# Strassen weight sums of a decoder layer: their loads and stores on GpSimd's queue, three buffers, an earlier load, and one half chunk less look-ahead

## The chip, the cores and the metric

The kernel runs on one core of a Trainium2 chip. A core has five engines that work side by side, each in its own order: TensorE (PE in the profile; its weight loads are PEld), VectorE (DVE), ScalarE (ACT), GpSimd (POOL) and SyncE (SP, which here only issues DMAs). The engines and the DMAs wait for each other by semaphores. The metric is the device time of one execution in microseconds, lower is better.

## The reference

One layer of a decoder on 256 tokens of width 2048, in float32. The parts, cut to what matters:

```python
h = rms_norm(x, attn_norm_g)
q, k, v, p = split(h @ w_in)                  # 3 x 1024 for 8 heads, 1024 for pooling
a = moba_attention(rms_norm(q), rms_norm(k), v, rel_bias)
m = multiscale_pool(p, pool_w, pool_scale)    # causal means over 2, 4, 8, 16 tokens
x = x + concatenate([a, m]) @ w_out
u = rms_norm(x) @ w_up                        # 2048 x 11264
y = conv_b + sum(conv_w[i] * shifted(u, i) for i in range(3))
gate, val = split(y)
x = x + (silu(gate) * val) @ w_down           # 5632 x 2048
```

With 256 tokens, all keys lie in one block, so the attention is plain causal attention with a bias.

## The kernel before

Every weight is used once, so the kernel is a stream of weights. A *step* is one half chunk of weights, 128 partitions by 1024 float32 columns; a chunk of two half chunks is one DMA of 1 MB into a `raw` tile (four of them, `RAWS`), issued by SP. TensorE multiplies in a reduced format, so each half chunk is split in two parts that are multiplied one after the other: ACT copies `raw` to `wh` (L169), DVE subtracts to get `wl` (L170). Activations are split in the same way. `split(i)` makes the part pair of half chunk i; `AHEAD` says how many half chunks the splits run ahead of TensorE, and `wpool` has `AHEAD + 1` buffers of `wh` and `wl`.

The order on all engines is written out by hand. The main loop at the end goes over the steps: first the splits that are due, then the step's matmuls, then its hooks, small pieces of work that `after(u, f)` hung on step u. Each engine does its share of this in that order. The steps:

- 0 to 47: six *token blocks* of eight steps for v, k and q (`tok_half`, L207). Attention hangs on them as hooks. At step 17 the attention's bias rows go out to DRAM as `band` and come back as `T`, both by POOL's queue.
- 48 to 63: the pooling columns (`feat_half`, L238 for `wh` with both activation parts, L240 for `wl` with one). 64 to 97: the output projection, which ends in the residual `x2`, its square sums on POOL (L638, L662) and, two steps into the next stage, `stats2`: a matmul `ps_row` (L348) that sums over partitions, from which the row scale `rrow` comes. `x2_T` transposes the residual on TensorE (L645).
- From step 98 (`UP0`) on, three *thirds* (`THIRDS`). Each has an up-projection, eight steps for each group of 256 hidden columns (four for the gate, a *gate block*, four for the value, a *value block*), and a down-projection. After each block comes its tail: `conv` (ACT L468, DVE `fs` L469, `u` L682, three taps on `y` L687 to L690), then for the gate the SiLU (L696), and for the value the product with the gate and its split into `hid` (L713 to L723). In the first half of a third's groups the tail also forms the seven combinations of the hidden columns for Strassen's scheme (*Strassen value blocks*).

Strassen's scheme replaces eight products of half-size blocks of `w_down` by seven, for which sums of weight blocks are needed. For 44 pairs of blocks (`NJ`) the kernel makes these sums itself, as *jobs*: `job_load` reads the four blocks (`job <- in_pairs`, 512 KB), `job_sums` makes four additions on DVE (L194), `job_store` writes the sums to DRAM (`tsum <- job`, 512 KB), from where the weight stream reads them in the down-projection (`raw <- tsum`). There is one `job` tile. The jobs are hung on *free* steps: 12 to 31, 64 to 97 and all steps of the up-projections. Job k takes the five free steps from the 5k-th on: load after the first, sums after the third, store after the fifth. Loads and stores stand in SP's queue among the weight loads.

Of the kernel before, what the change touches and what calls it, by code (L numbers as in the profile page):

```python
# [35 lines left out]
F32 = mybir.dt.float32  # L36
# [5 lines left out]
P = 128  # L42
D = 2048
S = 256
# [9 lines left out]
L = 384  # L54
CH = 2048
HALF = CH // 2
AHEAD = 5
RAWS = 4
BH = 768

# [4 lines left out]
UP0 = 98  # L65
# [43 lines left out]
def layer(ctx: ExitStack, tc: tile.TileContext, xT, wts, pairs, par, relT, ident_d, onehot_d, icnt_d, out):  # L109
    nc = tc.nc  # L110
    ctx.enter_context(tc.manual_schedule())
    keep = ctx.enter_context(tc.tile_pool(name="keep", bufs=1))
    wpool = ctx.enter_context(tc.tile_pool(name="wpool", bufs=AHEAD + 1))
    mm = ctx.enter_context(tc.tile_pool(name="mm", bufs=2, space=bass.MemoryType.PSUM))
# [11 lines left out]
    def small(name):  # L126
        return sm.tile([P, 512], F32, name=name, tag="small")
# [9 lines left out]
    offset, n = {}, 0  # L137
# [7 lines left out]
        first_part.setdefault(u, i)  # L145
    raws, wparts, tsum = {}, {}, {}

    def load(c, pieces=1, j=0, queue=None):

        if c not in raws:  # L150
            raws[c] = wpool.tile([P, CH], F32, name="raw", tag="raw", bufs=RAWS)
        r, k = raws[c], sched[chunk[c][0]]
        if k is None:
            w = HALF * len(chunk[c])
            o, n = j * w // pieces, w // pieces
            src = bass.AP(tensor=wts.tensor, offset=wts.offset + offset[c] + o, ap=[[w, P], [1, n]])
            (queue or nc.sync).dma_start(r[:, o:o + n], src)
        else:
            nc.sync.dma_start(r[:, :BH], pairs[k][:, HALF - BH:])
            nc.sync.dma_start(r[:, BH:BH + HALF], tsum.pop(k))  # L160
# [11 lines left out]
    def split(i):  # L172
        u, k = parts[i]
        split_piece(u, k, 0, HALF if sched[u] is None or k else BH)
        if u == chunk[chunk_of[u]][-1] and (k or sched[u] is None):
            release(chunk_of[u])

    def release(c):

        raws.pop(c)  # L180
        if c + RAWS < len(chunk):
            load(c + RAWS)


    job = {}

    def job_load(k):
        job["t"] = keep.tile([P, 4, S], F32, name="job", tag="job")
        nc.sync.dma_start(job["t"], pairs[k].rearrange("p (a n) -> p a n", n=S))

    def job_sums(k):
        t = job["t"]
        for o, a, b in ((1, 0, 1), (0, 0, 2), (2, 1, 2), (3, 2, 3)):
            nc.vector.tensor_tensor(t[:, o, :], t[:, a, :], t[:, b, :], op=OP.add)  # L194

    def job_store(k):
        tsum[k] = dram.tile([P, HALF], F32, name=f"tsum{k}")
        nc.sync.dma_start(tsum[k].rearrange("p (a n) -> p a n", n=S), job.pop("t"))

    def tok_half(u, act, k0, ps, first, last):  # L200

# [63 lines left out]
    def load_xT(k0, k1):  # L265

        c = slice(KT + k0 * S if k0 else 0, KT + k1 * S)
        nc.sync.dma_start(xboth[:, c], xT[:, c])

    def x_split(k0, k1):  # L270
        for k in range(k0, k1):
            g = xboth[:, k:k + 1]
            nc.scalar.activation(xh[:, k, 0, :], xin[:, k, :], AF.Copy, scale=g)
            nc.vector.scalar_tensor_tensor(xh[:, k, 1, :], xin[:, k, :], g,
                                           xh[:, k, 0, :].bitcast(F32), op0=OP.mult, op1=OP.subtract)

    nc.vector.memset(ones, 1.0)
    load(0, 4, 0, nc.scalar)  # L280
    ps = small("ps_start")
    for _ in range(7):
        nc.tensor.matmul(ps[:, :P], ones, ones, start=True, stop=True)
    nc.scalar.preload_act_table_set("natural_log_exp_and_others")

    for k in range(4):
        load_xT(k, k + 1)
        if k:
            load(0, 4, k)
    for u in range(2, 8):  # L290
        load_xT(2 * u, 2 * u + 2)
        load(u // 2, 2, u % 2)
# [3 lines left out]
    for c in range(2):  # L296
        release(c)
    for u in range(4, AHEAD):
        x_split(2 * u, 2 * u + 2)
# [266 lines left out]
    def after(u, f):  # L566

        hooks.append((u, f))
# [11 lines left out]

    for u in range(AHEAD, 8):
        pre[u - AHEAD] = lambda u=u: x_split(2 * u, 2 * u + 2)
    for a in range(4):
# [11 lines left out]
    for b in range(2):  # L595
# [3 lines left out]
        at = st["q", b, "end"] + 3  # L599
# [40 lines left out]
    def x2_T(i):  # L640

        t, k0 = i % NT, i // NT * 4
        ps = small("ps_x2t")
        for k in range(4):
            nc.tensor.transpose(ps[:, k * P:(k + 1) * P], late["x2"][:, k0 + k, t * P:(t + 1) * P], ident)  # L645
        nc.scalar.activation(late["x2t"][:, t, k0 * P:(k0 + 4) * P], ps, AF.Copy)
# [25 lines left out]
    f0 = len(steps)  # L672
# [72 lines left out]
                nc.sync.dma_start(out[:, ts, cs], x)  # L745

    HIDF = max(f * 14 * P + (g1 - g0 - f) * 4 * S for g0, g1, f in THIRDS)
    free = [*range(12, 32), *range(64, UP0)]
    for n, (g0, g1, f) in enumerate(THIRDS):
        free += range(len(steps), len(steps) + 8 * (g1 - g0))  # L750
        for g in range(g0, g1):
# [1 line left out]
            steps += feat_block(lambda: late["h"], XK, lambda ps, n=n, j=g - g0: value(ps, n, j))  # L753
        steps += down_order([down_block(n, b, n == 2) for b in range(D // 512)])
    for i in range(8):
        after(f0 + 1 + i // 2, lambda i=i: x2_T(i))
    for k in range(NJ):
        at = free[5 * k:]
        after(at[0], lambda k=k: job_load(k))
        after(at[2], lambda k=k: job_sums(k))  # L760
        after(at[4], lambda k=k: job_store(k))

    for u, f in hooks:
        steps[u].append(f)
    assert len(steps) == len(sched) and f0 == UP0, (len(steps), len(sched), f0)
    done = AHEAD
    for u in range(len(steps)):
        if u in pre:
            pre[u]()
        while done < min(first_part[u] + AHEAD + 1, len(parts)):  # L770
            split(done)
# [83 lines left out]
```

## Time and profile before

| | |
|---|---|
| median of three runs | 1199.75 us (1199.39 to 1199.9) |
| profiled execution | 1199.44 us, of which span 1197.6 us |
| mean granted TensorE clock | 0.952 |
| busy share of the span: PE, DVE, ACT, POOL | 90%, 71%, 47%, 5% |
| DMA | 263.96 MB, mean 220 GB/s |

How to read it: a row of waits says who waited for whom, the microseconds in total, how often and the longest. In a row of a group of instructions, the figures after the bar are its busy time, the mean of one in ns, and the idle time of its engine just before them with what ended it. A row of the timeline has its start from the beginning of the span, its length, and in brackets the idle time before it. A row of DMA issues has how many, the size of each, and the median time from issue to landing. The letter q after an engine's name means its queue (sequencer). A busy TensorE is not one at its peak, since matmuls are pipelined, and its clock is at times granted only at half speed.

### The profile page before, as it was taken

How to read it: one execution, taken by the hardware profiler on the slowest of the kernel's cores; microseconds unless marked ns; L12 is line 12 of the kernel's file. 1: busy time of each engine (PE TensorE's matmuls, PEld its weight loads, DVE VectorE, ACT ScalarE, POOL GpSimd, SP SyncE). 2: the span in 40 equal slices, each digit the busy share in tenths (PEclk: the TensorE clock that was granted, in tenths of full speed). 3: DMA queues.
4: the chain of work that ended last, by engine and by line, in shares of the span. 5: the costliest groups of instructions: out<-in, count | busy, mean ns of one | idle time of the engine just before them, and what ended most of it. 6: DMA issues, size and time to landing. Idle time of an engine off the chain costs nothing.

```text
span 1197.6 us, 15090 instructions
## 1 busy us (share of the span) xinstructions
PE 1080.0 (90%) x5836; PEld 927.5 (77%) x5836; DVE 850.9 (71%) x1187; ACT 564.7 (47%) x750; POOL 54.8 (5%) x44
## 2 busy tenths in 40 slices
PE   9968899999969989897899998898789999898898
PEld 7756688878858867776798887777678988786787
DVE  6815656875666787677788667768677867877885
ACT  7523354455345444443555434444355644544652
POOL 0300003501010000000000000000000000000000
PEclk9988899999989998998899998989989999998899
DMA  9767654476665657575777655647478765664583
GB/s 358 256 133 232 210 177 147 149 267 235 231 216 176 222 180 249 182 242 163 282 282 276 224 212 191 213 166 255 163 259 303 268 248 184 241 239 164 202 302 117
DMA packets 53865, 263.96 MB, mean 220 GB/s; under 512 B 6312, under 2 KB 7112, under 8 KB 34208
## 3 DMA queue, kind: packets, MB, share of 16 engines
q1 hardware_dynamic: 52656, 260.11, 61.9%
q0 software_dynamic: 992, 2.63, 1.4%
q8 instruction: 45, 0.74, 0.2%
q10 hardware_dynamic: 144, 0.26, 0.1%
q14 instruction: 28, 0.23, 0.1%
HBM read 236.23 MB, written 26.74 MB: 220 GB/s over the span
## 4 chain that ended last, share of the span: by engine, by line
PE 38%; DMA 26%; DVE 25%; ACT 4%; issue 4%; SPq 1%; POOL 1%; DVEq 0%; ACTq 0%; POOLq 0%
DMA job<-in_pairs 13%; DMA tsum<-job 12%; DVE wl L170 11%; PE ps_down L217 10%; PE ps_down L231 8%; PE ps_feat L238 8%; PE ps_tok L207 6%; PE ps_feat L240 4%; DVE job L194 4%; DVE y L690 2%; ACT wh L169 2%; DVE y L688 2%; DVE u L682 2%; DVE fs L469 1%; ACT y L687 1%
## 5 line engine op out<-in xcount | busy, mean ns | idle before, releaser
L170 DVE TENSOR_TENSOR wl<-raw,wh 128x1024 fp32r<-128x1024 f32 (+2 forms) x410 | 482.7, 1218 | 101.9 <-ACT wh L169 101.7
L238 PE MATMUL ps_feat<-x2h,wh 128*128 128x512 f32 x1408 | 514.6, 406 | 28.8 <-ACT wh L169 21.6
L169 ACT ACTIVATE wh<-raw 128x1024 fp32r<-128x1024 f32 (+2 forms) x410 | 401.8, 1019 | 121.1 <-PE ps_down L217 46.7
L240 PE MATMUL ps_feat<-x2h,wl 128*128 128x256 f32 x1408 | 407.2, 289 | 21.0 <-DVE wl L170 20.7
L238 PEld LDWEIGHTS ps_feat<-x2h,wh 128*128 128x128 f32 x1408 | 275.3, 196 | 95.6 <-ACT wh L169 26.6
L240 PEld LDWEIGHTS ps_feat<-x2h,wl 128*128 128x128 f32 x1408 | 275.4, 196 | 29.9 <-DVE wl L170 29.7
L194 DVE TENSOR_TENSOR job<-job 128x256 f32<-128x256 f32 x176 | 74.8, 425 | 132.9 <-DMA job<-in_pairs 128.4
L687 ACT ACTIVATE y<-u,pv 128x256 f32<-128x256 f32 x88 | 48.2, 595 | 217.6 <-DVE u L682 217.6
L231 PE MATMUL ps_down<-wh,hid 128*128 128x256 f32 x616 | 119.7, 296 | 13.3 <-ACT wh L169 13.3
L231 PEld LDWEIGHTS ps_down<-wh,hid 128*128 128x128 f32 x616 | 101.9, 201 | 15.1 <-ACT wh L169 14.2
L217 PE MATMUL ps_down<-wh,hid 128*128 128x512 f32 x352 | 111.5, 398 | 0.0
L207 PE MATMUL ps_tok<-wh,xh 128*128 128x512 f32 x384 | 110.3, 410 | 1.4 <-ACT wh L169 1.4
L231 PE MATMUL ps_down<-wl,hid 128*128 128x256 f32 x308 | 91.1, 296 | 6.6 <-DVE wl L170 6.6
L238 PE MATMUL ps_feat<-cat,wh 128*128 128x512 f32 x256 | 89.3, 392 | 3.0 <-DVE cat L513 3.0
L207 PEld LDWEIGHTS ps_tok<-wh,xh 128*128 128x128 f32 x384 | 73.8, 194 | 19.6 <-ACT wh L169 2.1
L217 PEld LDWEIGHTS ps_down<-wh,hid 128*128 128x128 f32 x352 | 65.9, 190 | 14.6
L240 PE MATMUL ps_feat<-cat,wl 128*128 128x256 f32 x256 | 71.8, 280 | 2.2 <-DVE wl L170 2.2
L207 PE MATMUL ps_tok<-wl,xh 128*128 128x512 f32 x192 | 61.8, 403 | 11.6 <-DVE wl L170 11.6
L217 PE MATMUL ps_down<-wl,hid 128*128 128x512 f32 x176 | 69.8, 397 | 0.0
L231 PEld LDWEIGHTS ps_down<-wl,hid 128*128 128x128 f32 x308 | 62.4, 203 | 8.1 <-DVE wl L170 8.1
L688 DVE SCALAR_TENSOR_TENSOR y<-u,pv,y 128x256 f32<-128x256 f32 x88 | 42.4, 482 | 29.7 <-ACT y L687 29.7
L238 PEld LDWEIGHTS ps_feat<-cat,wh 128*128 128x128 f32 x256 | 48.0, 188 | 13.8 <-DVE cat L513 3.3
(128 smaller groups left out, 796.7 us busy)
## 6 DMA issues: line engine op xcount, KB each, us to landing
raw<-in_wts SPq DMA_DIRECT2D x152, 1024.0 KB, 5.6
job<-in_pairs SPq DMA_DIRECT2D x44, 512.0 KB, 3.7
tsum<-job SPq DMA_DIRECT2D x44, 512.0 KB, 6.6
raw<-tsum SPq DMA_DIRECT2D x44, 512.0 KB, 5.0
raw<-in_pairs SPq DMA_DIRECT2D x44, 384.0 KB, 3.9
raw<-in_wts SPq DMA_DIRECT2D x12, 512.0 KB, 6.6
x<-in_xT SPq DMA_DIRECT2D x1, 2048.0 KB, 10.5
out<-x2t SPq DMA_DIRECT2D x8, 256.0 KB, 2.4
```

The costliest lines, as they stand in the source:

```text
L169: nc.scalar.activation(wh, w, AF.Copy)
L170: nc.vector.tensor_tensor(wl, w, wh.bitcast(F32), op=OP.subtract)
L194: nc.vector.tensor_tensor(t[:, o, :], t[:, a, :], t[:, b, :], op=OP.add)
L207: nc.tensor.matmul(ps[:, t, :], act[:, k0 + k, a, t * P:(t + 1) * P], w[:, ws], start=(first and k == 0 and n == 0), stop=(last and k == 1 ...
L217: nc.tensor.matmul(ps[:, t, :], act(a, k, t), w[:, k * 512:(k + 1) * 512], start=(first and k == 0 and n == 0), stop=(last and k == 1 and ...
L231: nc.tensor.matmul(dst[:, h * S:(h + 1) * S], z[:, a, slot, :], w[:, ws], start=(first and n == 0 and bank not in seen), stop=False, skip_ ...
L238: nc.tensor.matmul(ps, wh[:, ws], act[:, k, :, :], start=(first and n == 0), stop=False, skip_group_check=True)
L240: nc.tensor.matmul(ps[:, S:], wl[:, ws], act[:, k, 0, :], start=False, stop=(last and n == len(ks) - 1), skip_group_check=True)
L682: nc.vector.tensor_tensor(u[:, :, 2:], s, late["rrow"][:, None, :].to_broadcast([P, 2, S]), op=OP.mult)
L687: nc.scalar.activation(y[:, m, :], u[:, m, 2:], AF.Identity, scale=cw[2], bias=col(C_CB + f))
L688: nc.vector.scalar_tensor_tensor(y[:, m, :], u[:, m, 1:1 + S], cw[1], y[:, m, :], op0=OP.mult, op1=OP.add)
L690: nc.vector.scalar_tensor_tensor(y[:, m, :], u[:, m, :S], cw[0], y[:, m, :], op0=OP.mult, op1=OP.add)
```

## The change

Five things are changed together.

- The `job` tile gets three buffers, and the DMAs of a job are issued by POOL (`nc.gpsimd`) instead of SP.
- Free steps are now 68 to 97 and the up-projections. Job k starts at free step 9k/2 instead of 5k; its sums come six free steps after its load (before: two), its store one after the sums (before: two). So jobs overlap.
- `AHEAD` is 4 instead of 5: the splits run four half chunks ahead, and there are five buffers of `wh` and `wl` instead of six. This gives the space of two more `job` buffers.
- `x2_T` hangs two steps later.
- At the start the first weight piece is issued by SP instead of ACT, and ten instead of seven warm-up matmuls are made.

```diff
-AHEAD = 5
+AHEAD = 4
...
-    def load(c, pieces=1, j=0, queue=None):
+    def load(c, pieces=1, j=0):
...
-            (queue or nc.sync).dma_start(r[:, o:o + n], src)
+            nc.sync.dma_start(r[:, o:o + n], src)
...
     def job_load(k):
-        job["t"] = keep.tile([P, 4, S], F32, name="job", tag="job")
-        nc.sync.dma_start(job["t"], pairs[k].rearrange("p (a n) -> p a n", n=S))
+        job[k] = keep.tile([P, 4, S], F32, name="job", tag="job", bufs=3)
+        nc.gpsimd.dma_start(job[k], pairs[k].rearrange("p (a n) -> p a n", n=S))

     def job_sums(k):
-        t = job["t"]
+        t = job[k]
         for o, a, b in ((1, 0, 1), (0, 0, 2), (2, 1, 2), (3, 2, 3)):
             nc.vector.tensor_tensor(t[:, o, :], t[:, a, :], t[:, b, :], op=OP.add)

     def job_store(k):
         tsum[k] = dram.tile([P, HALF], F32, name=f"tsum{k}")
-        nc.sync.dma_start(tsum[k].rearrange("p (a n) -> p a n", n=S), job.pop("t"))
+        nc.gpsimd.dma_start(tsum[k].rearrange("p (a n) -> p a n", n=S), job.pop(k))
...
-    load(0, 4, 0, nc.scalar)
     ps = small("ps_start")
-    for _ in range(7):
+    for _ in range(10):
...
     for k in range(4):
         load_xT(k, k + 1)
-        if k:
-            load(0, 4, k)
+        load(0, 4, k)
...
-    free = [*range(12, 32), *range(64, UP0)]
+    free = [*range(68, UP0)]
...
     for i in range(8):
-        after(f0 + 1 + i // 2, lambda i=i: x2_T(i))
+        after(f0 + 3 + i // 2, lambda i=i: x2_T(i))
     for k in range(NJ):
-        at = free[5 * k:]
+        at = free[9 * k // 2:]
         after(at[0], lambda k=k: job_load(k))
-        after(at[2], lambda k=k: job_sums(k))
-        after(at[4], lambda k=k: job_store(k))
+        after(at[6], lambda k=k: job_sums(k))
+        after(at[7], lambda k=k: job_store(k))
```

What stands on the queues moves. SP before, in the first up-projection (L157 are weight loads, L189 the job's load, L198 its store):

```order
L157 DMA raw<-in_wts 128x2048 x2
L198 DMA tsum_2716<-job 128x1024
L189 DMA job<-in_pairs 128x1024
L157 DMA raw<-in_wts 128x2048 x2
L198 DMA tsum_2902<-job 128x1024
L157 DMA raw<-in_wts 128x2048
```

POOL now, from the end of the output projection into the first up-projection (the lines of the code have moved up by two; L636 and L660 are the square sums, L638 and L662 before):

```order
L636 TENSOR_TENSOR sq_1877<-sq_1877,xs 128x512
L198 DMA tsum_2650<-job 128x1024
L189 DMA job<-in_pairs 128x1024
L660 TENSOR_TENSOR sq_1877<-sq_1877 128x256
L198 DMA tsum_2817<-job 128x1024
L189 DMA job<-in_pairs 128x1024
L198 DMA tsum_2953<-job 128x1024
L189 DMA job<-in_pairs 128x1024
```

SP has only weight loads left there. On POOL, the load behind a store belongs to the job after next: a load is issued right behind the store of a job that started nine steps earlier.

On DVE the additions stand at other places and more densely. The last gate block of the first third, from its `u` to the `u` of the value block behind it, before:

```order
L682 TENSOR_TENSOR u_1917<-fs,rrow_2774 128x2x256
...
L690 SCALAR_TENSOR_TENSOR y<-u_1917,pv,y 128x256
L170 TENSOR_TENSOR wl<-raw,wh 128x1024
L170 TENSOR_TENSOR wl<-raw,wh 128x768
L170 TENSOR_TENSOR wl<-raw,wh 128x1024
L170 TENSOR_TENSOR wl<-raw,wh 128x768
L469 TENSOR_TENSOR fs<-ps_feat,fs 128x512
L682 TENSOR_TENSOR u_1918<-fs,rrow_2774 128x2x256
```

The same block now:

```order
L680 TENSOR_TENSOR u_1878<-fs,rrow_2721 128x2x256
...
L688 SCALAR_TENSOR_TENSOR y<-u_1878,pv,y 128x256
L170 TENSOR_TENSOR wl<-raw,wh 128x768
L170 TENSOR_TENSOR wl<-raw,wh 128x1024
L194 TENSOR_TENSOR job<-job 128x256 x4
L170 TENSOR_TENSOR wl<-raw,wh 128x768
L170 TENSOR_TENSOR wl<-raw,wh 128x1024
L467 TENSOR_TENSOR fs<-ps_feat,fs 128x512
L680 TENSOR_TENSOR u_1879<-fs,rrow_2721 128x2x256
```

A job's four additions have come into a block that had none, and the first `wl` is another half chunk, since the splits run one fewer ahead.

## The prediction

> **What bounds the kernel now.** I read the page first, then the list of waits, then sums by stage, and last the timeline inside single blocks. The page says that TensorE is busy 90% of the span, but its chain of work that ended last is mostly not TensorE:
>
> ```profile
> PE 1080.0 (90%) x5836; PEld 927.5 (77%) x5836; DVE 850.9 (71%) x1187; ACT 564.7 (47%) x750; POOL 54.8 (5%) x44
> ...
> PE 38%; DMA 26%; DVE 25%; ACT 4%; issue 4%; SPq 1%; POOL 1%; DVEq 0%; ACTq 0%; POOLq 0%
> ```
>
> A quarter of the span hangs on DMAs, another quarter on DVE. The waits name the DMAs, first DVE's, then SP's queue's:
>
> ```profile
> DVE job L194 <- DMA job<-in_pairs: 128.4, 36, 24.4
> ...
> SPq L189 <- DMA tsum<-job: 187.5, 34, 8.3
> ```
>
> With one `job` tile, SP holds each load until the store before it has landed, and DVE, which works in order, stands still until the load has landed: 128.4 us in 36 of 44 jobs. Nothing is slow in itself:
>
> ```profile
> job<-in_pairs SPq DMA_DIRECT2D x44, 512.0 KB, 3.7
> tsum<-job SPq DMA_DIRECT2D x44, 512.0 KB, 6.6
> ```
>
> DVE makes the `wl` half of every weight, so its standstill reaches TensorE when the look-ahead is used up. By stage (columns: PE, PEld, DVE, ACT, POOL busy, granted clock, DMA share): 60 to 180 us are the token blocks with jobs; at 334.8 the first third's up-projection begins; 362.6, 673.6 and 983.6 are the first gate's `u` of each third, 569.8, 882.6 and 1126.1 the last `u`.
>
> ```profile
> 60.00:180.00 120.00, 98.63 (x426) 79.94 (x425) 55.99 (x99) 43.74 (x66) 2.14 (x3) 0.90 0.62 189
> 180.00:334.80 154.80, 147.64 (x866) 129.44 (x865) 108.72 (x159) 72.81 (x116) 34.29 (x25) 1.00 0.59 205
> 334.80:362.60 27.80, 18.03 (x97) 15.29 (x96) 17.37 (x24) 14.15 (x22) 4.16 (x3) 0.82 0.64 224
> 362.60:569.80 207.20, 184.21 (x993) 157.60 (x992) 151.16 (x224) 94.19 (x125) 0.00 (x0) 0.95 0.59 202
> ...
> 673.60:882.60 209.00, 184.98 (x991) 157.68 (x990) 150.81 (x224) 90.90 (x120) 0.00 (x0) 0.94 0.58 199
> ...
> 983.60:1126.10 142.50, 132.62 (x737) 114.25 (x736) 107.21 (x158) 66.55 (x88) 0.00 (x0) 0.96 0.59 206
> ```
>
> In the three up stretches the bound is DVE's chain, and a single block shows it. From one `u` to the next DVE does a convolution tail, four `wl` and the next `fs`; TensorE needs four steps of eight matmul pairs. The rows: a gate block without a job, a Strassen value block without a job, and two matmul pairs.
>
> ```profile
> 789.84 0.69 DVE L682 TENSOR_TENSOR u<-fs,rrow 128x512 f32<-128x512 f32 x1
> ...
> 800.03 0.69 DVE L682 TENSOR_TENSOR u<-fs,rrow 128x512 f32<-128x512 f32 x1
> ...
> 717.72 0.69 DVE L682 TENSOR_TENSOR u<-fs,rrow 128x512 f32<-128x512 f32 x1
> ...
> 730.13 0.69 DVE L682 TENSOR_TENSOR u<-fs,rrow 128x512 f32<-128x512 f32 x1
> ...
> 454.64 0.39 PE L238 MATMUL ps_feat<-x2h,wh 128*128 128x512 f32 x1
> ...
> 454.99 0.39 PE L238 MATMUL ps_feat<-x2h,wh 128*128 128x512 f32 x1
> ```
>
> Gate block 10.2 us, value block 12.4; TensorE 4 x 8 x 0.35 = 11.2 a block. A gate and a value block are 22.6 on DVE against 22.4 on TensorE, before any job. A job adds four additions of 0.425 us (the rows below), 1.70 us, and its wait. So in these stages DVE is the longer one with jobs even when no load is late, and the time a stage gives up is the wait it loses, less the jobs it gains.
>
> **The change, part by part.**
>
> Up stages. The sums on DVE in the same three stretches, last figures the idle time before them:
>
> ```profile
> L194 DVE TENSOR_TENSOR job<-job 128x256 f32<-128x256 f32 x48 | 20.4, 425 | 22.0 <-DMA job<-in_pairs 20.8
> L194 DVE TENSOR_TENSOR job<-job 128x256 f32<-128x256 f32 x48 | 20.4, 425 | 29.4 <-DMA job<-in_pairs 28.1
> L194 DVE TENSOR_TENSOR job<-job 128x256 f32<-128x256 f32 x28 | 11.9, 425 | 13.0 <-DMA job<-in_pairs 12.3
> ```
>
> Six steps at 2.8 us are 17 us for a load that lands in 3.7, so I take all of these waits as gone. Jobs move in from steps 12 to 31: by the new order 14, 13 and 9 lie in the stretches instead of 12, 12 and 7. That gives -20.8 + 2 x 1.7 = -17.4, -28.1 + 1.7 = -26.4 and -12.3 + 2 x 1.7 = -8.9 us. The stretches become 189.8, 182.6 and 133.6, all still above TensorE's 15, 15 and 11 blocks of 11.2 (168, 168, 123), which is why I take the whole wait and no more.
>
> Token blocks. Jobs leave steps 12 to 31. TensorE's waits there, and the three stretches at half clock that follow them:
>
> ```profile
> PE ps_tok L207 <- DVE wl L170: 11.6, 1, 11.6
> PE ps_T L407 <- DVE qn L398: 5.9, 1, 5.9
> PE ps_T L407 <- DVE kn L398: 3.9, 1, 3.9
> ...
> 83.10:93.30 10.20, 2.83 (x7) 2.25 (x8) 5.72 (x8) 0.00 (x0) 0.00 (x0) 0.50 0.60 134
> 96.70:103.50 6.80, 5.68 (x18) 4.81 (x19) 2.19 (x2) 3.08 (x4) 0.77 (x1) 0.50 0.93 303
> 127.40:134.20 6.80, 4.41 (x15) 3.83 (x16) 4.31 (x7) 4.32 (x6) 0.00 (x0) 0.50 0.84 292
> ```
>
> Waits 21.4; 12.9 us of matmuls at half clock would take 6.5 less. Together -27.9 if nothing else is late there (rival below). From 180 to 334.8 TensorE idles 154.8 - 147.6 = 7.2 us in all; I take -2 of it.
>
> Entry to the up-projection. `stats2` on TensorE waited for a chain that began behind a job's wait on DVE:
>
> ```profile
> PE ps_row L348 <- ACT x2t L646: 8.7, 1, 8.7
> ...
> 344.76 1.80 DVE L194 TENSOR_TENSOR job<-job 128x256 f32<-128x256 f32 x4 [3.88 <-DMA job<-in_pairs]
> ...
> 347.61 0.68 DVE L469 TENSOR_TENSOR fs<-ps_feat,fs 128x512 f32<-128x512 f32 x1
> ...
> 353.06 1.19 PE L348 MATMUL ps_row<-sq,ones 128*128 128x256 f32 x2 [8.71 <-ACT x2t L646]
> ```
>
> With DVE on time, `fs` of the last output block needs no more than two steps to reach `ps_row`, and the first gate's `u` comes after four steps (11.2), `ps_row` (1.2), the ACT copy and `fs` (0.7 each): 13.8 us instead of the stretch's 27.8. I take -13.5. The transposes `x2_T`, two steps later now, then fall beside the first gate's tail; ACT copies them between its `wh`, as before, so nothing for that move.
>
> One half chunk less. Where DVE is the bound it never waits for a free `wh`/`wl` buffer, so nothing there. At the three entries to the down-projection the last value block's tail holds the splits while TensorE lives on split parts: four instead of five, half a Strassen step, 21 x 0.12 / 2 = 1.3 us each by this row of the chain, +3.8.
>
> ```profile
> 594.43 10.08 PE ps_down L231 x84
> ```
>
> Start. The first weight piece goes from ACT's queue to SP's, behind one issue more; the row has two in 0.86, so +0.4. Three more warm-up matmuls run in that time.
>
> ```profile
> 0.74 0.86 SPq L268 DMA_DIRECT2D xboth<-in_xT  x2
> ```
>
> GpSimd's queue. 88 DMAs move past SP's weight loads to POOL. On POOL they stand among its additions for `stats2` ; a store there waits for DVE's sums, and behind it wait the next load, due nine steps later, and the next addition, whose input comes later on DVE anyway. The nearest rows for their price are the two `T` loads that POOL already issues, 512 KB too, and a DVE instruction beside one of them:
>
> ```profile
> T<-band POOLq DMA_DIRECT2D x2, 512.0 KB, 7.7
> band<-rsb POOLq DMA_DIRECT2D x1, 1536.0 KB, 36.8
> ...
> 96.69 0.78 POOL L328 DMA_DIRECT2D T<-band  x1 [36.08 <-DMA band<-rsb]
> ...
> 96.54 1.23 DVE L398 TENSOR_TENSOR kn<-ps_tok,hr 128x1024 f32<-128x1024 f32 x1
> 97.68 1.22 DVE L170 TENSOR_TENSOR wl<-raw,wh 128x1024 fp32r<-128x1024 f32 x1
> ```
>
> 0.78 us of POOL, 7.7 us to landing, DVE's `kn` beside it at 1.23, as long as the `wl` of the same width after it, 1.22. Cost to DVE: 0 by these rows. Upper end: beside a POOL addition a `wl` took 1.54 instead of 1.22:
>
> ```profile
> 336.27 1.54 DVE L170 TENSOR_TENSOR wl<-raw,wh 128x1024 fp32r<-128x1024 f32 x1 [1.71 <-ACT wh L169]
> ```
>
> 0.3 x 72 issues in the up stretches = +22. Lower end: nothing below, since the blocks above, with four `wl` in a row, leave no room for weight loads that SP issues too late. I take 0, since the `kn` row has the same kind of instruction on POOL.
>
> The Trainium skill ("SBUF — State Buffer", "Who interferes with whom") says that a DVE instruction with two SBUF inputs is held up by a GpSimd one that reads SBUF, not by one that only writes, and infers that making descriptors needs the write side: by that the sum keeps its 0, and both rows agree. Its box on DMAs from GpSimd's queue advises against them, because their descriptors wait while DVE copies in a two-port mode; by that loads land late, but the sum stays unless they are later than 17 us.
>
> Sum: -17.4 - 26.4 - 8.9 - 27.9 - 2 - 13.5 + 3.8 + 0.4 = -91.9. The profiled execution took 1199.44 (span 1197.6 and 1.84 around it), 0.3 below the runs' median 1199.75. 1199.4 - 91.9 = 1107.5; I say 1107.
>
> **The rivals.**
>
> Descriptors cost DVE: the +22 above, 1129. For it the slowed `wl`; against it the `kn` row. 12%.
>
> The token blocks stall all the same: `band` takes 36.8 us from 59 on, and in that time a weight load took 10.5 us, while TensorE uses one up in two steps, 5.6:
>
> ```profile
> raw<-in_wts SPq DMA_DIRECT2D x4, 1024.0 KB, 10.5
> ```
>
> If the weights, not the job's load behind them, are late, the 11.6 us wait and part of the half clock stay: +13, 1120. Against it: six half chunks were loaded and unsplit when DVE stopped, enough for 17 us more. 10%.
>
> The look-ahead decides: with four parts instead of five TensorE stands a step of 2.8 us at each of the 22 value blocks, because DVE waits for buffers there: +62, 1169. Against it: DVE's chain explains each up stretch without any wait for TensorE. 5%.
>
> The queue is the trouble, slower than before: every DMA of the new queue takes as long as `band`. A tile is free again after load, sums and store, 36.8 + 1.7 + 36.8 = 75.3 us for three jobs, 25 a job against the 4.5 steps at 3 us = 13.7 that are there; 36 jobs in the stretches then wait 11 us each, +400, about 1500. It turns against the kernel from 2.1 us of wait a job (92/44), a period of 15.8, or a landing of 23 us. For it: only `band` and `T` are known of this queue; against it, `T` of the same size took 7.7. 5%. The Trainium skill ("DMA: Bandwidth & Descriptors", "Issuing engines are not separate DMA queues") says that all queues share the same 16 DMA engines and that another issuer saves only issue time; by that the gain can come only from the look-ahead, as in the sum.
>
> More than the sum: with less delay on DVE the gaps at the three down entries close as well, some 5 us each: 1092. 8%.
>
> **How the numbers follow.** 60% for the forecast, 1107, with its own range 1096 to 1118. The rest as given. The range 1088 to 1140 holds forecast, the first two rivals and most of the last, about 8 in 10 after the doubt in each price. Within 0.2% (2.4 us, about what a measurement of this kernel can tell) 1%; slower 4%, from the queue; faster 95%.
>
> **What would show it.** DVE's wait for `job` near 0 in the profile after, stretches between first and last `u` of 190, 183 and 134 us, `ps_row` without a wait, no half clock before 300 us, T-like landings (4 to 9 us) for `job` and `tsum` on POOL, `wl` at 1.2 us. It is wrong if `wl` or the additions lengthen, if DVE waits for `job` or ACT for `raw`, or if TensorE's pace, not DVE's, sets the up stretches.

## The result, and the profile after

The changed kernel takes 1098.72 us (median of four runs, 1097.87 to 1100.3) against 1199.83 before (1199.39 to 1204.67): ratio 0.915, 95% interval 0.9125 to 0.9176. The forecast was 1107, in the range 1088 to 1140. The profiled execution took 1097.87 us, its span 1096.1.

First the shares on the page, then the DMA issues and the groups of the additions and of `wl`. Line numbers have moved up by two behind L300.

```profile
PE 1048.8 (96%) x5842; PEld 907.3 (83%) x5842; DVE 851.6 (78%) x1187; ACT 565.4 (52%) x750; POOL 100.6 (9%) x132
...
PE 56%; DVE 27%; ACT 7%; issue 6%; DMA 3%; POOL 1%; DVEq 0%; ACTq 0%; SPq 0%; POOLq 0%
...
L170 DVE TENSOR_TENSOR wl<-raw,wh 128x1024 fp32r<-128x1024 f32 (+2 forms) x410 | 485.9, 1220 | 126.0 <-ACT wh L169 125.8
...
L194 DVE TENSOR_TENSOR job<-job 128x256 f32<-128x256 f32 x176 | 74.5, 424 | 4.5
...
job<-in_pairs POOLq DMA_DIRECT2D x44, 512.0 KB, 7.0
tsum<-job POOLq DMA_DIRECT2D x44, 512.0 KB, 3.3
```

DMA's share of the chain of work that ended last went from 26% to 3%; DVE's stayed. The additions no longer wait for a load: 4.5 us of idle time before 176 of them, and no releaser named. Their loads take longer than before (7.0 us instead of 3.7), and nobody notices. `wl` takes 1220 ns on average (1218 before) and an addition 424, so POOL's DMA issues slow neither. One by one the trace says the same: the 68 full-width `wl` beside which POOL issued a DMA took 1219 ns on average, the 267 beside which POOL did nothing took 1221, and the 23 beside which POOL computed took 1910.

By stage (columns as in the prediction): the token blocks from 60 us on, the entry to the up-projection (first matmul on `x2h` to the first gate's `u`), then the up stretches with the first two down-projections between them.

```profile
60.00:152.10 92.10, 91.42 (x421) 74.61 (x420) 51.45 (x86) 42.98 (x66) 1.55 (x2) 1.00 0.64 191
205.60:301.60 96.00, 94.96 (x563) 83.73 (x562) 74.13 (x102) 52.52 (x74) 14.76 (x21) 1.00 0.73 266
301.60:315.20 13.60, 13.60 (x83) 12.08 (x82) 10.82 (x15) 7.39 (x11) 3.12 (x4) 1.00 0.82 286
315.20:507.20 192.00, 179.43 (x1014) 155.00 (x1014) 153.91 (x232) 96.47 (x129) 14.85 (x28) 0.98 0.64 233
507.20:607.80 100.60, 95.82 (x567) 85.07 (x566) 79.90 (x88) 54.48 (x60) 1.06 (x2) 0.97 0.75 272
607.80:789.60 181.80, 173.21 (x985) 150.19 (x984) 151.80 (x228) 91.08 (x120) 13.73 (x26) 0.99 0.67 241
789.60:890.60 101.00, 96.74 (x571) 85.99 (x571) 79.88 (x88) 54.45 (x60) 1.05 (x2) 0.97 0.76 281
890.60:1024.00 133.40, 128.63 (x730) 111.26 (x729) 110.44 (x167) 66.88 (x88) 8.48 (x16) 0.99 0.64 229
```

The three up stretches are 192.0, 181.8 and 133.4 us, forecast were 189.8, 182.6 and 133.6. The token blocks run at full clock with TensorE 91.42 of 92.10 us busy. In the up stretches TensorE still idles 12.6, 8.6 and 4.8 us: DVE is the longer one there, as forecast.

### The profile page after: what moved, and what is told of

It is laid out like the page before. It is cut to its first block, busy times and chain, and to the rows that moved or that the text cites. A ratio compares the mean times of both kernels' runs of the same rounds, so it can differ in the third digit from the quotient of the medians.

```text
span 1096.1 us, 15271 instructions
## 1 busy us (share of the span) xinstructions
PE 1048.8 (96%) x5842; PEld 907.3 (83%) x5842; DVE 851.6 (78%) x1187; ACT 565.4 (52%) x750; POOL 100.6 (9%) x132
## 4 chain that ended last, share of the span: by engine, by line
PE 56%; DVE 27%; ACT 7%; issue 6%; DMA 3%; POOL 1%; DVEq 0%; ACTq 0%; SPq 0%; POOLq 0%
PE ps_feat L238 15%; DVE wl L170 12%; PE ps_down L217 11%; PE ps_down L231 9%; PE ps_tok L207 9%; PE ps_feat L240 8%; ACT wh L169 4%; DVE y L688 3%; DVE y L686 3%; DVE u L680 2%; DMA raw<-in_wts 2%; DVE fs L467 2%; ACT y L685 2%; DVE job L194 2%; DMA x<-in_xT 1%
## 5 line engine op out<-in xcount | busy, mean ns | idle before, releaser
L170 DVE TENSOR_TENSOR wl<-raw,wh 128x1024 fp32r<-128x1024 f32 (+2 forms) x410 | 485.9, 1220 | 126.0 <-ACT wh L169 125.8
L238 PE MATMUL ps_feat<-x2h,wh 128*128 128x512 f32 x1408 | 496.6, 396 | 7.3 <-ACT wh L169 7.3
L240 PE MATMUL ps_feat<-x2h,wl 128*128 128x256 f32 x1408 | 398.6, 283 | 14.1 <-DVE wl L170 14.0
L238 PEld LDWEIGHTS ps_feat<-x2h,wh 128*128 128x128 f32 x1408 | 267.1, 190 | 68.3 <-ACT wh L169 10.1
L240 PEld LDWEIGHTS ps_feat<-x2h,wl 128*128 128x128 f32 x1408 | 267.1, 190 | 21.0 <-DVE wl L170 20.7
L207 PE MATMUL ps_tok<-wh,xh 128*128 128x512 f32 x384 | 107.1, 400 | 0.0
L198 POOL DMA_DIRECT2D tsum<-job x44 | 23.8, 541 | 680.9 <-DVE job L194 668.1
L207 PEld LDWEIGHTS ps_tok<-wh,xh 128*128 128x128 f32 x384 | 71.3, 188 | 17.5 <-ACT wh L169 0.8
L231 PEld LDWEIGHTS ps_down<-wl,hid 128*128 128x128 f32 x308 | 61.2, 199 | 4.2 <-DVE wl L170 4.1
```

The source lines that it names most:

```text
L170: nc.vector.tensor_tensor(wl, w, wh.bitcast(F32), op=OP.subtract)
L198: nc.gpsimd.dma_start(tsum[k].rearrange("p (a n) -> p a n", n=S), job.pop(k))
L207: nc.tensor.matmul(ps[:, t, :], act[:, k0 + k, a, t * P:(t + 1) * P], w[:, ws], start=(first and k == 0 and n == 0), stop=(last and k == 1 ...
L231: nc.tensor.matmul(dst[:, h * S:(h + 1) * S], z[:, a, slot, :], w[:, ws], start=(first and n == 0 and bank not in seen), stop=False, skip_ ...
L238: nc.tensor.matmul(ps, wh[:, ws], act[:, k, :, :], start=(first and n == 0), stop=False, skip_group_check=True)
L240: nc.tensor.matmul(ps[:, S:], wl[:, ws], act[:, k, 0, :], start=False, stop=(last and n == len(ks) - 1), skip_group_check=True)
```

## Experiments

All runs are summed up in one table. "Ahead" is the time from the start to the first gate's `u`, "up" the sum of the three up stretches, "rest" the two down-projections between them and the tail after the third, to DVE's last instruction (all read off the timeline of the profiled execution; the span ends some 3 us later, with the last store). The wait is DVE's for `job`. Ratios are against runs of the kernel before on the same chip. In the names, sp and pool say which queue issues a job's DMAs, the number behind them how many buffers there are, and a5 that `AHEAD` is 5.

| run | median us | ratio, 95% interval | wait for `job` | ahead | up | rest |
|---|---|---|---|---|---|---|
| before | 1199.83 | | 128.4 | 362.6 | 558.8 | 272.9 |
| after | 1098.72 | 0.915, 0.9125 to 0.9176 | 0 | 315.2 | 507.2 | 270.7 |
| e_sp3 | 1097.98 | 0.9111, 0.9089 to 0.9132 | 0 | 315.7 | 505.8 | 271.0 |
| e_pool1 | 1130.46 | 0.9377, 0.935 to 0.9405 | 27.9 | 332.0 | 523.2 | 270.2 |
| e_sp1 | 1129.95 | 0.9379, 0.9354 to 0.9405 | 29.5 | 326.4 | 527.0 | 269.7 |
| e_queue | 1131.6 | 0.939, 0.9355 to 0.9425 | 53.3 | 353.7 | 500.9 | 271.0 |
| e_sp1a5 | 1164.32 | 0.9673, 0.9643 to 0.9703 | 64.5 | 325.3 | 559.5 | 269.1 |
| e_pool1a5 | 1116.81 | 0.9261, 0.9235 to 0.9287 | 20.2 | 327.7 | 517.0 | 268.0 |
| e_dve | 1056.05 | 0.8751, 0.8735 to 0.8767 | 0 | 316.4 | 466.9 | 268.8 |
| e_tok | 1105.21 | 0.9167, 0.9147 to 0.9188 | 14.5 | 327.4 | 501.9 | 271.6 |
| e_ahead3 | 1121.55 | 0.9303, 0.9279 to 0.9326 | 0 | 319.3 | 523.2 | 277.0 |
| e_x2old | 1098.83 | 0.9136, 0.911 to 0.9162 | 0 | 317.4 | 505.7 | 270.7 |
| best1 | 1077.68 | 0.8933, 0.8917 to 0.8948 | 0 | 324.7 | 477.7 | 270.3 |
| best2 | 1068.91 | 0.8884, 0.8864 to 0.8905 | 0 | 320.3 | 468.0 | 275.7 |

### Queue or buffers

The prediction gave the gain to the early load and nothing to the queue. Two theories are set against each other: L, the look-ahead over three buffers decides; Q, the queue decides, because on SP a job's store and load stand behind weight loads that wait for a free `raw` buffer. The kernel before shows that such rows exist (SP's queue and DVE):

```profile
400.98 1.81 DVE L194 TENSOR_TENSOR job<-job 128x256 f32<-128x256 f32 x4 [1.54 <-DMA job<-in_pairs]
404.32 0.42 SPq L198 DMA_DIRECT2D tsum<-job  x1
414.15 0.33 SPq L157 DMA_DIRECT2D raw<-in_wts  x1
414.53 0.42 SPq L189 DMA_DIRECT2D job<-in_pairs  x1
```

The sums end at 402.79, their store goes out 1.5 us later, and the next load 10 us after that: 7.4 us until the store has landed, as the one tile needs it, and 2.8 us more behind a weight load.

**Three buffers on SP (e_sp3).**

```diff
-        nc.gpsimd.dma_start(job[k], pairs[k]...)
+        nc.sync.dma_start(job[k], pairs[k]...)
...
-        nc.gpsimd.dma_start(tsum[k]..., job.pop(k))
+        nc.sync.dma_start(tsum[k]..., job.pop(k))
```

> The changed kernel, but a job's load and store are issued by SP again; three buffers, the six steps between load and sums, and the free steps stay. Theory L (the early load decides: 17 us of lead are more than any landing seen): DVE does not wait for job, up stretches of about 192, 182 and 133 us, time 1099 to 1106. Theory Q (the queue decides: in the kernel before, a job's load stood on SP behind weight loads that wait for a free raw buffer, one of them 14 us long): the loads are late again, DVE waits 2 to 4 us in most of the 44 jobs, time 1150 to 1190.

1097.98 us. The ratios of e_sp3 and after have overlapping intervals. DVE has no wait for `job`:

```profile
L194 DVE TENSOR_TENSOR job<-job 128x256 f32<-128x256 f32 x176 | 74.5, 423 | 4.5
...
job<-in_pairs SPq DMA_DIRECT2D x44, 512.0 KB, 7.1
tsum<-job SPq DMA_DIRECT2D x44, 512.0 KB, 6.5
```

So with three buffers and six steps of lead the queue is worth nothing. In the changed kernel a load has landed at least 9.2 us before its sums start, on SP at least 8.0 (the smallest of all 44 jobs). It also lands in 7.1 us on SP: the longer landing comes with the new times, not with the queue.

**One buffer on POOL (e_pool1) and on SP (e_sp1).** e_pool1 is after with

```diff
-        job[k] = keep.tile([P, 4, S], F32, name="job", tag="job", bufs=3)
+        job[k] = keep.tile([P, 4, S], F32, name="job", tag="job")
...
-        after(at[6], lambda k=k: job_sums(k))
-        after(at[7], lambda k=k: job_store(k))
+        after(at[2], lambda k=k: job_sums(k))
+        after(at[3], lambda k=k: job_store(k))
```

and e_sp1 is the same with both DMAs on `nc.sync`.

> The changed kernel with one job buffer: sums two steps after the load, store one step after the sums, on GpSimd's queue as now. Theory L (look-ahead over three buffers decides): the load lands 7.0 us after its issue, so DVE waits in most jobs, 2 to 4 us each as before (3.6 in 36 jobs), time 1150 to 1190. Theory Q (the queue decides): on POOL nothing stands between sums, store and the next load, so store 3.3 + load 7.0 + two issues of 0.6 = 11.5 us fit into the 4.5 steps of about 3.1 us = 14 us between two jobs; no wait for job, time 1099 to 1108.

> The changed kernel with one job buffer (sums two steps after the load, store one after the sums) and the job's DMAs on SP: neither the queue nor the buffers, only the new free steps, four half chunks of look-ahead and the start. Both theories expect the waits of the kernel before, 3.6 us in most of now 44 jobs, while the token blocks stay free of them: 1098.7 plus 80 to 140, so 1165 to 1240.

Both take 1130 us, so both theories missed e_pool1, one on each side, and e_sp1 came out 35 us below what all expected. The additions in e_pool1, and below them those in e_sp1:

```profile
L194 DVE TENSOR_TENSOR job<-job 128x256 f32<-128x256 f32 x176 | 74.7, 424 | 32.6 <-DMA job<-in_pairs 27.9
```

```profile
L194 DVE TENSOR_TENSOR job<-job 128x256 f32<-128x256 f32 x176 | 74.9, 426 | 34.4 <-DMA job<-in_pairs 29.5
```

Neither part of the change is needed to lose most of the wait: other steps, a store one step earlier and four parts take it from 128.4 to 29.5 us. Of the 128.4, four waits of 41.4 us lay in the token blocks, where no job is left; which of the other differences took the rest was not separated. On POOL the wait shows up at a second place. POOL works in order, and with one buffer its load of the next job stands until the store has landed; behind it stands the last square sum, for which `ps_row` waits at the entry of e_pool1:

```profile
323.54 0.54 POOL L189 DMA_DIRECT2D job<-in_pairs  x1 [2.65 <-DMA tsum<-job]
324.09 0.73 POOL L660 TENSOR_TENSOR sq<-sq 128x256 f32<-128x256 f32 x1
324.88 1.22 PE L346 MATMUL ps_row<-sq,ones 128*128 128x256 f32 x2 [6.38 <-POOL sq L660]
```

**The queue alone (e_queue).** The kernel before, with only the two DMAs of a job on `nc.gpsimd`.

> The kernel before with one edit: a job's load and store are issued by GpSimd's queue. Theory Q: in the up stages the chain of 11.5 us fits into the five steps of about 3.1 us between two jobs, so the 61 us of waits there go; in the token blocks a job's load now stands behind the 36.9 us of band in the same queue, so one job's sums hold DVE for 30 to 40 us and TensorE for 15 to 25; time 1120 to 1150. Theory L: one buffer, so the waits stay; time 1195 to 1215.

Theory Q's numbers hold here. The three up stretches:

```profile
353.70:543.50 189.80, 178.93 (x995) 155.25 (x994) 150.72 (x225) 94.32 (x125) 12.89 (x24) 0.97 0.63 223
645.90:826.70 180.80, 174.39 (x991) 150.99 (x991) 150.01 (x224) 90.99 (x120) 12.84 (x24) 0.99 0.65 230
926.90:1057.10 130.20, 127.22 (x731) 111.39 (x731) 106.91 (x157) 66.66 (x88) 6.96 (x13) 0.99 0.62 220
```

They are 57.9 us shorter than before (558.8 - 500.9), with the same jobs at the same steps. DVE's waits there went from 61.2 (20.8 + 28.1 + 12.3) to 3.2: 58.0 less. A wait taken from DVE came out of the time one for one. What the median job (9 to 44) shows, from the rows of the timeline: in the kernel before 2.7 us from the end of the sums to the issue of the store, 6.7 from there to the next load, 3.7 to its landing, 13.1 in all; in e_queue 0.3 + 4.2 + 5.1 = 9.6. The 3.5 us between them are nearly the 3.6 that DVE had waited in each of 36 jobs. They have two sources: the store goes out 2.4 us sooner, since no weight load stands ahead of it (before, 11 of these 36 stores went out more than 3 us after their sums, in e_queue 2), and it lands in 3.9 us instead of 6.6; the load takes back 1.4. Why the store lands sooner on POOL's queue no run shows.

The rest of e_queue is lost ahead of the up-projection, where jobs still lie in the token blocks. The additions there, and POOL:

```profile
58.38 1.10 POOL L322 DMA_DIRECT2D band<-rsb  x1 [3.87 <-DVE rsb L321]
60.29 0.55 POOL L189 DMA_DIRECT2D job<-in_pairs  x1 [0.81 <-DMA tsum<-job]
96.00 1.80 DVE L194 TENSOR_TENSOR job<-job 128x256 f32<-128x256 f32 x4 [33.55 <-DMA job<-in_pairs]
```

A job's load issued behind `band` landed when `band` did, 35 us later, and DVE stood 33.55 us. The queue is not all of it: in the kernel before, the load that SP issued at 64.72, while `band` was under way, landed 22.6 us later. POOL's own `T` is held as well: it goes out at 102.28, behind a job's load that waits for its store, 7.7 us after `band` has landed.

So three buffers with the lead remove the waits, and in the up stretches the queue alone nearly does as well; together they give no more. That does not agree with the sentence of the Trainium skill ("DMA: Bandwidth & Descriptors", "Issuing engines are not separate DMA queues") that another issuer saves only the time of issuing, which the prediction put beside its zero for the queue. Where a queue holds instructions that wait, another issuer also saves what stands ahead in it; here that and the store's shorter landing are worth 58 us.

### What one buffer leaves to chance (e_sp1a5, e_pool1a5)

The two kernels with one buffer, with `AHEAD = 5` instead of 4.

> The kernel with one job buffer on SP and the new free steps (1130), with the splits five half chunks ahead instead of four. Prediction's term: 1.3 us at each of three entries to the down-projection less, 1126. Theory F (from four on look-ahead is free; only the step to three made DVE wait for TensorE, 23 us): within 3 us of 1130. Rival (each half chunk counts as much as the step from four to three): 1105 to 1110.

> One job buffer on GpSimd's queue (1130 with the splits four half chunks ahead), with five instead of four. On SP this step cost 34 us, all of it in DVE's waits for job (64.5 us instead of 29.5). Theory O (with five, the weight loads that wait for a free raw buffer stand at other places around a job's load and store in SP's queue, and one buffer has no slack for that): on POOL's queue no weight load stands there, so 1126 to 1133 and waits near 28 us. Rival (the splits one further ahead shift the sums on DVE against their loads, whichever queue issues them): 1150 to 1165.

On SP one half chunk more costs 34 us, which nobody had expected. DVE's wait for `job` is 35.0 us longer (64.5 - 29.5), which is all of it. On POOL the same step gains 14 us. So the loss hangs on the queue and not on DVE's order, as theory O said; its forecast of no difference on POOL missed. Three rows of SP's queue and one of DVE in e_sp1a5 show one such job:

```profile
645.22 13.08 SPq L157 DMA_DIRECT2D raw<-in_wts  x2
658.35 0.43 SPq L198 DMA_DIRECT2D tsum<-job  x1
665.05 0.33 SPq L189 DMA_DIRECT2D job<-in_pairs  x1
...
668.79 1.81 DVE L194 TENSOR_TENSOR job<-job 128x256 f32<-128x256 f32 x4 [3.52 <-DMA job<-in_pairs]
```

The store goes out 1.5 us after the sums, behind two weight loads, lands in 6.7, the load in 3.7, and DVE is there 3.5 us sooner. With one buffer this chain runs once per job with nothing to spare, and it is decided by which weight loads happen to stand around it. Between four and five the traces speak for SP's order and against the landing times: on average of jobs 9 to 44 a load lands in 5.0 us in both, a store in 5.3 and 5.2, but from the store's landing to the next load's issue it takes 4.2 us in e_sp1a5 and 2.6 in e_sp1. The order was not varied by itself.

### What bounds the up stretches (e_dve)

```diff
-        for o, a, b in ((1, 0, 1), (0, 0, 2), (2, 1, 2), (3, 2, 3)):
+        for o, a, b in ((1, 0, 1),):
```

> The changed kernel with only the first of a job's four additions (the other three sums are left out, so the down-projection multiplies wrong weights): 1.27 us of DVE less per job, nothing else moved. Theory (DVE's chain sets the up stretches): gate and Strassen value block together 22.6 + 2 x 0.42 = 23.4 us, gate and plain value block below TensorE's 22.4; stretches of about 175, 168 and 124 us instead of 192, 182 and 133, time 1055 to 1065. Rival (TensorE's pace sets them): at most 3 us less, 1095 to 1099.

1056.05 us. The three stretches:

```profile
316.40:492.70 176.30, 171.88 (x993) 151.08 (x992) 136.27 (x192) 97.19 (x129) 14.86 (x28) 0.99 0.69 251
593.00:760.80 167.80, 166.95 (x966) 146.61 (x965) 135.53 (x189) 91.62 (x120) 13.73 (x26) 1.00 0.71 260
861.40:984.30 122.90, 122.55 (x712) 107.83 (x711) 99.07 (x139) 67.02 (x88) 8.47 (x16) 1.00 0.69 250
```

40.3 us less in the stretches (507.2 - 466.9), of 36 x 1.27 = 45.7 us of additions left out there. In the second and third TensorE is now busy 166.95 of 167.8 us and 122.55 of 122.9: its own pace (15 and 11 blocks of 11.2 = 168 and 123) is the floor there; the first holds a gate block of 18.7 us. So DVE's chain set the stretches of the changed kernel, at 507.2 us against 459 for all 41 blocks at TensorE's pace.

### The token blocks (e_tok)

```diff
-    free = [*range(68, UP0)]
+    free = [*range(12, 32), *range(68, UP0)]
```

> The changed kernel with steps 12 to 31 among the free steps again, so that four to five jobs lie in the token blocks, with three buffers and six steps of lead, on GpSimd's queue. Theory B (moving the jobs away from band gave the token term): loads behind the 36.9 us of band land 10 to 20 us after their sums are due, TensorE loses 5 to 20 us there, the up stretches give 4.4 x 1.7 = 7.5 us: 1097 to 1112. Rival (the lead covers the token blocks too): 1098.7 - 7.5 = 1091.

Theory B holds: the up stretches gain 5.3 us (507.2 - 501.9), the part ahead loses 12.2. The third job's load was issued at 62.78, 3.4 us behind `band` in POOL's queue, and landed at 104.20, 41.4 us later. In the rows of POOL and DVE:

```profile
59.39 1.10 POOL L320 DMA_DIRECT2D band<-rsb  x1 [17.47 <-DVE rsb L319]
...
62.78 0.53 POOL L189 DMA_DIRECT2D job<-in_pairs  x1
...
104.23 1.80 DVE L194 TENSOR_TENSOR job<-job 128x256 f32<-128x256 f32 x4 [14.46 <-DMA job<-in_pairs]
```

Three buffers and six steps of lead do not cover the 36.9 us of `band`. But they cover much of what jobs cost there: the token blocks end at 162.2 us, against 179.5 before and 152.1 in the changed kernel. Without jobs they end at 152.4 even with one buffer on SP (e_sp1). So taking the jobs out of those steps is enough for the whole token term, and the rest of the change would have given 17.3 of its 27.4 us without that. The queue is no part of these 17.3: in e_queue, with one buffer, the token blocks end at 179.7.

### Look-ahead (e_ahead3)

```diff
-AHEAD = 4
+AHEAD = 3
```

(The first four splits, made before the loop, stay.)

> The changed kernel with the splits three half chunks ahead instead of four (four buffers of wh and wl). Prediction's term, once more: half a Strassen step, 1.3 us, at each of three entries to the down-projection, 1102 to 1103. Theory F (look-ahead is free where DVE is the bound, as the entries measured after suggest): within 2 us of 1098.7. Rival (look-ahead decides): DVE waits for buffers, a step of 2.8 us at each of 22 value blocks, 1160.

1121.55 us, 18 us more than after by the ratios, 23 by the times. Neither my 3.9 nor F's 2 us, nor the rival's 62. 16 us of it are in the up stretches (523.2 - 507.2). ACT's copy ahead of `fs` waits for TensorE now; first the row of waits of e_ahead3, then that of the changed kernel:

```profile
ACT fs L466 <- PE ps_feat L240: 100.2, 52, 4.7
```

```profile
ACT fs L466 <- PE ps_feat L240: 20.2, 14, 1.8
```

With three parts in hand TensorE has not finished a block when ACT, and behind it DVE, come to it, so the two bounds, as I read these rows, partly add up instead of overlapping. Four is enough where nothing else waits: e_queue has five and, in stretches with only 3.2 us of waits, 500.9 us, against 507.2 - 5 x 1.7 = 498.7 for the changed kernel with four, whose stretches hold five jobs more (36 against 31). With one buffer on POOL, where DVE does wait, the fifth was worth 14 us.

### The transposes (e_x2old)

```diff
-        after(f0 + 3 + i // 2, lambda i=i: x2_T(i))
+        after(f0 + 1 + i // 2, lambda i=i: x2_T(i))
```

> The changed kernel with x2_T hung two steps earlier again, as before the change. Prediction (the move costs nothing): within 1.5 us of 1098.7. Theory X (the move made the first gate block longer, 18.5 us instead of 15.4, since ACT's copies now stand in front of its wh): 1095 to 1097. Rival (the copies then stand ahead of stats2's chain on ACT and make ps_row late, as its 8.7 us wait for x2t before): entry 2 to 6 us longer, 1101 to 1105.

1098.83 us: no difference. The entry is 1.5 us longer and the first stretch 1.6 shorter. Entry and first gate block are 32.1 us together in both. That `x2_T` makes this block long (18.5 us) is likely but was not tried alone: best2 below, which takes six of the eight out, has 11.2 us there, but has also moved the job whose additions lay in the block. In e_dve, with three of those four additions gone, the block still takes 18.7 us, so they are not the cause.

### Jobs where DVE has room (best1, best2)

If a job costs 1.70 us of time in an up stretch only because DVE is the bound there, it should cost nothing in a down-projection (DVE busy 80 of 100.6 us) or in the token blocks behind `band`. best1 is e_sp3 with the loads at steps

```diff
-    for k in range(NJ):
-        at = free[9 * k // 2:]
+    D0, U1, D1, U2 = UP0 + 64, UP0 + 96, UP0 + 160, UP0 + 192
+    start = [*range(34, 98, 4)]
+    start += [*range(D0 - 5, D0 + 27, 4), *range(U1 + 2, U1 + 58, 7)]
+    start += [*range(D1 - 3, D1 + 29, 4), *range(U2 + 2, U2 + 30, 7)]
```

sums six steps later and stores seven. best2 takes other steps for the sums, and six of the eight `x2_T` into the output projection:

```diff
+    at = [36, 39, 42, 45, 48, 54, 60, 66, 72, 78, 84, 90, D0 - 26, D0 - 18, D0 - 10]
+    at += [D0 + 2 + 7 * i // 2 for i in range(9)] + [U1 + 36, U1 + 43, U1 + 50, U1 + 57]
+    at += [D1 + 2 + 3 * i for i in range(10)] + [U2 + 12, U2 + 20, U2 + 27, U2 + 33, U2 + 39, U2 + 45]
+    start = [u - 6 for u in at]
...
-        after(f0 + 3 + i // 2, lambda i=i: x2_T(i))
+        after(o0 + 13 + 8 * (i // 2) + 2 * (i % 2) if i < 6 else f0 + 2 * i - 11, lambda i=i: x2_T(i))
```

> The changed kernel with the jobs moved to where DVE has room (and their DMAs on SP, which made no difference): jobs 0 to 15 from step 34 on, one every four steps; eight in each of the first two down-projections; eight and four in the second and third up-projection; still six steps from load to sums. Theory (a job costs 1.7 us in an up stretch and nothing where DVE idles): first stretch at TensorE's pace, about 172 instead of 192; second and third with six to eight jobs less, 172 and 126 instead of 182 and 133; 1060 to 1070. Rival (the additions are only paid elsewhere: DVE is busy 80 of 100 us in a down-projection, and TensorE waits for parts there): down-projections 5 to 14 us longer each, 1080 to 1095.

> The spread jobs of 1077.7 placed again by the room that the profile showed: sparser in the pooling and output projection, three in the plain half of the first up-projection, nine and ten in the first two down-projections, four in the plain half of the second up-projection and six in the third; and six of the eight x2_T in the output projection, where ACT has room, instead of in front of the first gate's wh. Theory: pooling, output projection and entry lose their 3 us each again, the first gate block (18.5 us) comes to about 12, the second up stretch to 170, the third to 126: 1058 to 1066. Rival (the added jobs in the down-projections, DVE then busy 92 of 100 us, make TensorE wait): 4 to 10 us of it given back, 1066 to 1078.

best1 takes 1077.68 us, faster than both kernels but 8 us above what was expected: the up stretches give 29.5 us, the part ahead takes back 9.5. From the end of the token blocks to the first matmul on `x2h` TensorE idles 6.9 us instead of 2.0, and the entry is 2.9 us longer. One thing that slows DVE there is POOL: while it computes for the pooling columns an addition takes up to 1.41 us instead of 0.42, and three jobs take 4.5 to 5.3 us instead of 1.8. One of them, and what POOL does beside it:

```profile
169.33 5.83 POOL L477 TENSOR_TENSOR pa<-pa 128x512 f32<-128x512 f32 x4
...
172.41 4.46 DVE L194 TENSOR_TENSOR job<-job 128x256 f32<-128x256 f32 x4
```

So a job is not free wherever DVE has idle time. best2 takes 1068.91. Its first and second up stretch, and the two down-projections:

```profile
320.20:489.90 169.70, 168.54 (x976) 147.78 (x975) 136.11 (x189) 93.05 (x122) 0.00 (x0) 1.00 0.55 201
590.50:760.00 169.50, 169.10 (x985) 148.98 (x984) 137.66 (x194) 91.37 (x120) 0.00 (x0) 1.00 0.57 207
...
489.90:590.50 100.60, 97.31 (x582) 86.52 (x581) 90.59 (x120) 53.92 (x60) 0.00 (x0) 0.98 0.94 352
760.00:866.60 106.60, 98.29 (x571) 85.67 (x570) 92.25 (x124) 53.42 (x60) 0.00 (x0) 0.97 0.91 338
```

Both stretches are within 2 us of TensorE's 168. Nine jobs in the first down-projection are free (100.6 us, as in the changed kernel, with DVE busy 91 instead of 80); ten, closer together, in the second cost 5.6 us (106.6 against 101.0). That is the rival's give-back, and best2 came out 3 us above its theory.

## Why the prediction was right, and where it was not

Against the sum of 1107.5 the profiled execution is 9.6 us lower. By its own terms:

- **Up stretches**, forecast 506.0 in all: 507.2. Right, and e_dve and e_queue show both halves of the reason (DVE's chain is the bound, the wait comes out one for one). Within it the first is 2.2 us too long, by a first gate block of 18.5 us.
- **Token blocks**, -27.9 + 0.4: their end went from 179.5 to 152.1, -27.4. Right: 20.7 us of it are idle time of TensorE (from 60 us on, 21.4 before and 0.7 now), and no half speed is left there. e_sp1 shows that leaving those steps is enough for it; e_tok shows that it was not the only way, as the rest of the change gives 17.3 us of it with the jobs still there. The start, +0.4, cost nothing: the first product with `wl` comes at 6.3 us, 6.5 before.
- **Entry**, -13.5: 27.8 to 13.6, -14.2, and `ps_row` has no wait. The move of `x2_T` at nothing: right by e_x2old.
- **Pooling and output projection**, -2: from 155.3 to 149.5, -5.8. Mis-sized: I took 2 of 7.2 us of idle time without a reason in the rows, and TensorE idles only 1.0 us of the output projection now.
- **One half chunk less**, +3.8 at the down entries: the first down-projection is 3.2 us shorter (a wait for `job` at its entrance is gone too), the second the same, the tail to the end of the span 0.6 longer. Mis-sized: it is nothing here. TensorE's waits at the three entries are as long with four parts as they were with five; the row of waits after, then before:

```profile
PE ps_down L231 <- ACT wh L169: 12.7, 3, 4.6
```

```profile
PE ps_down L231 <- ACT wh L169: 13.3, 4, 4.1
```

  The step took it that a fifth part was in hand when the last value block's tail began. Where DVE is the bound, TensorE has eaten it by then. When that block's `u` began, TensorE had started the last matmul of the up-projection 9.3, 6.1 and 5.1 us earlier with five parts, 6.1, 4.9 and 4.4 us earlier with four; and at the second and third entry it ran out of parts 1.6 us after this `u` with five, 1.4 us with four. One step further, in e_ahead3, the price is 18 to 23 us.
- **GpSimd's queue at nothing**: right for this kernel, by 1220 ns for `wl` and by e_sp3. The rule of the Trainium skill that had been put beside it ("SBUF — State Buffer", "Who interferes with whom") agrees: `wl` and the additions both have two inputs in SBUF, and neither grew beside 88 issues; its other half, the hold-up beside a GpSimd instruction that reads SBUF, shows in the 23 `wl` of 1910 ns and in the additions of best1. The `kn` row, on which I had put the zero, could not tell: of its two inputs only `hr` lies in SBUF, the other is `ps_tok`, where TensorE's products are (a PSUM tile in the kernel). My sentence on POOL's order, that a held DMA there delays nothing, holds only with three buffers: with one, `ps_row` waited 6.4 us for POOL.

Against the sum the up stretches are 1.2 us longer, the token blocks with the start 0.1 longer, the entry 0.7, the pooling and output projection 3.8 and the down-projections 6.4 us shorter: these are the 9.6 us. So the two mis-sized terms, both on the same side, make the miss.

One reason failed although the number held. "By that the gain can come only from the look-ahead" is wrong: in the up stretches the queue alone gives 57.9 us. The waits were due to a chain of store and load that stood among waiting weight loads, and either part of the change breaks it. That the prediction's number held in spite of this is because its lead removes the same waits.

Of the rivals, the descriptors, the slow queue and the look-ahead did not happen. `band` did no harm because no job lies near it; e_tok and e_queue show it would have. The last one, closing gaps at the down entries, is not what made up the 9.6 us.

## What to carry to other kernels

A DMA that stands in a queue behind others that wait for buffers is late by their wait, not by its own length: look for what stands ahead of it, and then give it either a queue without such waits or more buffers and a lead that covers what stands ahead. Here both together gave no more than one; and an in-order engine that takes over DMAs passes the wait on to its own work (`ps_row`, `T`). When the wait is gone, ask what the work itself costs in that stage: here moving additions from stages where DVE is the bound to ones where it idles, with six transposes, gave another 30 us. Idle time alone is not room, though: look for what runs beside it, as POOL's additions did in best1.

## What the runs showed of the hardware that was not expected

- A 512 KB load on POOL's queue landed in 7.0 us in the changed kernel, but on SP's, at the same steps, in 7.1, where it had taken 3.7 before; with one buffer it took 5.8 and 5.5. The store took 3.3 on POOL and 6.5 on SP. So at the same steps the queue makes no difference to the load and 3.2 us to the store, and the load's time changes with the steps at which it is issued. Why was not tried.
- TensorE's longer waits come with half speed: each of the 13 waits over 3 us in the two kernels has such a stretch around or right behind its end. For the 4.58 us at the first down entry, which began at 508.1, the granted clock of the changed kernel reads

```profile
510.40:517.20 6.80, 4.32 (x18) 4.03 (x19) 6.03 (x8) 5.88 (x7) 0.00 (x0) 0.50 0.31 127
```

  Such stretches, of 3.4 us or a multiple of it, made 113 us in the kernel before and 34 after, the end of the span left out. In the token blocks, where the half speed went with the waits, 27.4 us were gained for 20.7 us of idle time, as the prediction had it.
